# Loading x first, a first block of conditioning on TensorE, 1024-column loads and chunks of 3, 4, 4, 5 in a fused encoder layer

## Chip, core and metric

The kernel runs on one core of one Trainium2 chip. The metric is device microseconds (us) for one execution: the median of several. The engines are TensorE (PE in the profile; PEld is its loading of weights), VectorE (DVE), ScalarE (ACT), GpSimd (POOL) and SyncE (SP), whose queue issues nearly all transfers from HBM. Each engine works through its own queue strictly in order.

## What is computed

One layer on 256 tokens of 2048 channels in float32. The part that matters here is its beginning:

```python
cond = silu(c)                                   # [1, 2048]
mod = cond @ w_mod + b_mod                       # [1, 6*2048]
sh1, sc1, gt1, sh2, sc2, gt2 = split(mod, 6)
u = rms_norm(x, norm1_g) * (1 + sc1) + sh1       # [256, 2048]
aq, ak, av, rq, rf, ri, rg, ga, gr = split_columns(u @ w_in)
ya = diff_attention(aq, ak, av, lam)             # 8 heads
yr = hgrn2(rq, rf, ri, rg, lower_bounds)         # 8 heads, gated recurrence
m = sigmoid(ga) * (ya @ w_att_out) + sigmoid(gr) * (yr @ w_rec_out)
x = x + gt1 * (m @ w_o)
x = x + gt2 * swiglu(rms_norm(x, norm2_g) * (1 + sc2) + sh2)
```

followed by a last RMS norm. `w_mod` has 100 MB, `w_in` 92 MB; all weights together are read once.

## The kernel before

Every product of weights and activations is exact to float32 by splitting both into two parts (`wh`, `wl` and `uH`, `uL`): ScalarE rounds a loaded weight tile to `wh` (line 229), VectorE subtracts to get `wl` (line 231), and TensorE multiplies three times (lines 239 to 241) for each 128 channels ("block"), 512 columns and 128 tokens. With two token tiles a block costs 6 products for 512 columns.

Phase 1 computes seven column groups of `w_in` (`first_cols`: RF, RQ, RI, AQ, AK, AV, RG, each 1024 wide, so 84 products for each of the 16 blocks). A block of `u` needs its scale and shift first, and these need 2048 x 128 values of `w_mod` twice. So phase 1 goes by chunks of blocks (`kchunks`, here 3, 5, 4, 4): while the products of one chunk run, `mod_cols` sums the scales and shifts of the next. It loads rows of `w_mod` (tile `wm`, or `w` for the first chunk), VectorE multiplies them by `cond` and accumulates in `modc` (lines 390 and 394: one instruction for each of 16 row blocks and for scale and shift, 32 in all), TensorE sums `modc` over partitions (`pmc`, line 320, two trace records for each product), VectorE adds the bias (`sh_col`, `sc_col`, lines 403 to 405), and `modulated` makes `u`, `uH` and `uL` (lines 356, 366, 367). How many steps of this go between the products is set by `pace["cond"]`.

`group` does 512 columns at a time in two of the four PSUM banks tagged `acc`; in the first chunk ScalarE copies the banks to `part` (line 434), in later chunks VectorE adds them (line 436). In the last chunk the steps of `hgrn_scores` run beside the products. Phase 2 (the gates, attention, the merge, the SwiGLU) isn't touched.

Before the first chunk the kernel transposes c into `cond`, loads x and normalises it (`norm1`: eight squares on ScalarE, line 328; reciprocal root on VectorE; `xn`, line 343; transposes `pxT`, line 346; copies to `xT`), and loads the small vectors (`rows`, `brows`, lines 142 to 155), which TensorE transposes (`pc`) to give `cols` and `bcols`. The first chunk's loads of `w_mod` stand around the load of x in SP's queue. The tile framework orders the instructions of each engine; buffers rotate: three of `w`, three of `wm`, four each of `wh` and `wl`.

Of the kernel before, what the change touches and what calls it, by code (L numbers as in the profile page):

```python
# [42 lines left out]
XAT, XAT2 = 4, 4  # L43
PACE2, PACE3, PACES, PACE1 = 0.7, 1.6, 2.2, 1.5
kchunks = [(0, 3), (3, 5), (8, 4), (12, 4)]

# column starts of the combined input projection
# [4 lines left out]
def block_kernel(  # L52
# [46 lines left out]
    def make_masks():  # L99
        # mask[L][s, (b, l)] = 1 where key row s lies in the lower half of the 2L-block b  # L100
        for lv in range(7):
            L = 1 << lv
            nb = 64 // L
            m = const.tile([P, 64], F32, name=f"mask{L}")
            nc.gpsimd.memset(m, 1.0)
            mv = m.rearrange("p (b l) -> p b l", l=L)
            nc.gpsimd.affine_select(out=mv, in_=mv, compare_op=ALU.is_ge, fill=0.0,
                                    base=0, pattern=[[-2 * L, nb], [0, L]], channel_multiplier=1)
            nc.gpsimd.affine_select(out=mv, in_=mv, compare_op=ALU.is_ge, fill=0.0,
                                    base=L - 1, pattern=[[2 * L, nb], [0, L]], channel_multiplier=-1)  # L110
            masks[L] = m

# [9 lines left out]
    def quarter(tiles, g):  # L122
        """Columns g*512.. of a row kept in two tiles."""
        return tiles[g // 2][:, (g % 2) * NG:(g % 2 + 1) * NG]
# [37 lines left out]
    def small_params():  # L162
        # lower bound: softmax of the logits over depth, its first cumulative sum
# [12 lines left out]
        # lam on every partition  # L176
# [7 lines left out]
        # lam[:, 0] = lambda, lam[:, 1] = -lambda  # L184
# [4 lines left out]
    def rstd_of(ssq, n, width, name, eps=None):  # L189
        """1 / sqrt(ssq / width + eps), [P, n]: a bit-level first guess and Newton's steps."""  # L190
# [30 lines left out]
    def load_mod(k0, nk, n0, ncol, own):  # L221
        """Rows of w_mod; the first ones go where later the other weights do."""
        return load(w_mod, k0, nk, n0, ncol, wpool.tile([P, nk, ncol], F32, tag="wm", name="wm", bufs=NM) if own else None)

    def split(w, j, n, c0):
        """The parts of w[:, j:j+n, c0:c0+512]."""
# [7 lines left out]
    def products(po, aH, aL, k, wh, wl, kk, first, last, tiles=(0, 1)):  # L234
        """po[t] += a[:, k, t].T @ w[:, kk], in three passes."""
# [19 lines left out]
    def step():  # L255
        """Work beside the products: some of it after every load of weights."""
# [10 lines left out]
    def gemm(ap, kt, n0, aH, aL, k00=0, tail=0):  # L267
        """[256, 512] columns n0.. of a @ w in two banks; the last `tail` channel blocks are done for
        the first 128 tokens before the others."""
# [20 lines left out]
    def halves(tiles):  # L290
        """[P, k, 256] kept in tiles of four k."""
        return lambda k, ts: tiles[k // 4].rearrange("p (k s) -> p k s", s=S)[:, k % 4, ts]

# [1 line left out]
    def mod_rows(name, chunk):  # L295
        """Steps: acc[p, n] = sum over k of cond * w_mod (+ bias on row 0), then its sum over p."""
# [14 lines left out]
    def row_sum(a):  # L311
        """The sums of a's columns, on every partition, in place."""
# [19 lines left out]
    def norm1(xt):  # L332
        s8 = small.tile([P, 2, 4], F32, tag="s8", name="ssq")
        for t in range(2):
            for g in range(4):
                square_sum(s8[:, t, g:g + 1], quarter(xt[t], g))
        s2 = small.tile([P, 2], F32, tag="s2", name="ssq1")
        nc.vector.reduce_sum(out=s2, in_=s8, axis=AX.X)
        rr = rstd_of(s2, 2, D, "n1")
        for g in range(4):  # L340
            for t in range(2):
                xn = tmpt("xn")
                nc.vector.tensor_scalar_mul(out=xn, in0=quarter(xt[t], g), scalar1=rr[:, t:t + 1])
                p = bank("pxT")
                for j in range(4):
                    nc.tensor.transpose(out=p[:, j * P:(j + 1) * P], in_=xn[:, j * P:(j + 1) * P], identity=ident)  # L346
                nc.scalar.copy(out=xT[g].rearrange("p (k s) -> p k s", s=S)[:, :, t * P:(t + 1) * P], in_=p.rearrange("p (k s) -> p k s", s=P))
# [13 lines left out]
    def modulated(src, k, H, L):  # L361
        """H + L = src * sc + sh for the k-th 128 channels."""
# [11 lines left out]
    def mod_cols(k0, nk, chunk, gcol, src, H, L, after=None):  # L374
        """Steps: shift and scale of a norm for channels k0*128.., straight into columns, and then
        the norm's output for these channels."""
        wid = nk * P
        a = [tmp.tile([P, 1024], F32, tag="modc", name=f"modc{ci}", bufs=2) for ci in range(2)]
        own = chunk + k0 > 0
# [19 lines left out]
        for _ in range(GAP if chunk else GAP1):  # L399
            yield  # L400
        ks = slice(k0, k0 + nk)
# [4 lines left out]
        if src is not None:  # L406
            for k in range(k0, k0 + nk):
                modulated(src(k, slice(0, S)), k, H, L)

# [6 lines left out]
    def group(ci, col, g, pieces, last):  # L416
        """Adds the products of pieces (k, nk, parts, column in the parts) to columns col + g*512.."""
        po = [acc_ps.tile([P, NG], F32, tag="acc", name=f"acc{t}") for t in range(2)]
        for i, (k, nk, w, c0) in enumerate(pieces):
            if w is None:  # L420
                w = load(w_in, k, nk, col + g * NG, NG)
            for j in range(0, nk, SK):
                n = min(SK, nk - j)
                wh, wl = split(w, j, n, c0)
                for kk in range(n):
                    products(po, uH, uL, k + j + kk, wh, wl, kk, i == 0 and j + kk == 0,
                             i == len(pieces) - 1 and j + kk == nk - 1)
            step()
        if ci == 0:
            part[col][g] = bigt(f"part{col}").rearrange("p (t n) -> p t n", t=2)  # L430
        for t in range(2):
            d = part[col][g][:, t]
            if ci == 0:
                nc.scalar.copy(out=d, in_=po[t])
            else:
                nc.vector.tensor_add(out=d, in0=po[t], in1=d)
            if last and col == RG:
                nc.scalar.activation(d, d, AF.Sigmoid)

    def mods1(ci):  # L440
        k0, nk = kchunks[ci]
        return mod_cols(k0, nk, 0, g1c, xTv, uH, uL)

    def chunk_cols(ci):
        k0, nk = kchunks[ci]
        full = [(q, 4) for q in range(k0, k0 + nk - nk % 4, 4)]
        rest = nk % 4
        nsteps = 14 * (len(full) + (1 if rest else 0))
        pace["cond"] = 0.0
        if ci + 1 < len(kchunks):  # L450
            cond_side.append(mods1(ci + 1))
            pace["cond"] = AHEAD * 2 * len(mod_loads(kchunks[ci + 1][1])) / nsteps
        last = ci == len(kchunks) - 1
        order = [(col, g) for col in first_cols for g in range(2)]
        if last:
            assert rest in (0, 3)
            order[:4] = [(RF, 0), (RQ, 0), (RF, 1), (RQ, 1)]
        shared = None
        for i, (col, g) in enumerate(order):
            pieces = [(k, n, None, 0) for k, n in full]  # L460
            if rest in (1, 2):
                if g == 0:
                    shared = load(w_in, k0 + nk - rest, rest, col, 1024)
                pieces.insert(len(pieces) if g == 0 else 0, (k0 + nk - rest, rest, shared, g * NG))
            elif rest:
                pieces.append((k0 + nk - rest, rest, None, 0))
            group(ci, col, g, pieces, last)
            if last:
                pace["side"] = PACE1
            if last and (col, g) == (RQ, 0):  # L470
                side.append(hgrn_scores(0))
            if last and (col, g) == (RQ, 1):
# [4 lines left out]
    def transpose4(src):  # L477
        """[128 tok, 4*128] -> a bank [128, 4, 128 tok]."""
# [5 lines left out]
    def split_store(H, L, k0, t, pv, scale=None, bscale=None):  # L484
        """Transposed [128, 4, 128 tok] (in PSUM) times a column -> the parts H, L of k0.."""
# [13 lines left out]
    def normed_heads(po, gate, name, eps=None):  # L499
        """[128 tok, 4 heads, 128] in PSUM -> times rstd per head (and the gate), natural."""  # L500
# [23 lines left out]
    def hgrn_scores(hh):  # L524
        """Four heads. Decays between a query and a key are products of f over the tokens between
        them; a pair is taken at the level L whose 2L-block holds both, in different halves. Within
        L-blocks qa = q times f up to and with the query's token, kb = (1 - f) times f after the
        key's token, T = the product of f over the block."""
# [15 lines left out]
        # the pairs of a token with itself  # L544
# [11 lines left out]
        for lv in range(8):  # L556
# [5 lines left out]
            if L < 128:  # L562
# [5 lines left out]
                # to blocks of twice the length  # L568
# [43 lines left out]
    def attention(hh):  # L612
# [6 lines left out]
        for t in range(2):  # L619
# [3 lines left out]
            for hp in range(2):  # L623
# [16 lines left out]
                # s0 * (p0 / s0 - lam * p1 / s1): the norm of the head takes s0 out again  # L640
# [31 lines left out]
    first = mods1(0)  # L672
    for _ in range(XAT):
        next(first)
    x1 = load_x()
    load_rows()
    for _ in range(XAT2):
        next(first, None)
    norm1(x1)
    for _ in first:  # L680
        pass
    for ci in range(len(kchunks)):
# [202 lines left out]
```

## Time and profile before

| | us |
|---|---|
| median of 3 runs | 1566.48 (1564.33 to 1570.16) |
| profiled execution, span | 1566.1 |
| PE busy in it | 1502.2 (96%) |
| DVE busy | 1105.5 (71%) |
| ACT busy | 729.2 (47%) |

The span is the time from the first to the last instruction of one profiled execution; it is the time of that execution, and lies 0.4 us below the median. Products overlap in the trace (one lasts 390 ns while the next starts earlier), so counts and starts tell more than busy time.

### The profile page before, as it was taken

What the parts mean: (1) busy time and instruction counts of PE and PEld (TensorE: products, weight loads), DVE (VectorE), ACT (ScalarE), POOL (GpSimd) and SP (SyncE); (2) the same over time, 40 slices, a digit from 0 to 9 for tenths busy, and PEclk for the clock granted to TensorE, in tenths of its full rate; (3) what the DMA queues carried; (4) which work ended last, traced back from release to release, by engine and by line L of the source; (5) the groups of instructions that cost most, each with busy time, mean ns of one, the idle gap of its engine ahead of it and who ended that gap; (6) DMA issues with size and microseconds to landing.
All of it is one profiled execution on the core that took longest, in us unless ns stands there. A gap on an engine that the chain in (4) does not pass through costs nothing.

```text
span 1566.1 us, 18325 instructions
## 1 busy us (share of the span) xinstructions
PE 1502.2 (96%) x6931; PEld 1236.2 (79%) x6931; DVE 1105.5 (71%) x1443; ACT 729.2 (47%) x1003; POOL 10.5 (1%) x40
## 2 busy tenths in 40 slices
PE   1989999999999999999989999999999999999997
PEld 1767888888877778788868888788888888888886
DVE  6768889688877688888558877869655444454555
ACT  3554353534466764344345545444333444444443
POOL 1000000000000000000000000000000000000000
PEclk9999999999999999999989999999999999999999
DMA  8888989634664479889648998859655655565652
GB/s 302 284 278 302 311 275 324 206 129 148 232 241 160 135 249 339 312 321 344 206 137 291 334 327 284 315 192 321 205 190 195 194 195 189 190 191 196 207 188 107
DMA packets 175282, 373.67 MB, mean 239 GB/s; under 512 B 8237, under 2 KB 12502, under 8 KB 175194
## 3 DMA queue, kind: packets, MB, share of 16 engines
q1 hardware_dynamic: 174936, 372.42, 69.6%
q8 instruction: 54, 0.88, 0.2%
q14 instruction: 34, 0.28, 0.1%
q10 hardware_dynamic: 258, 0.09, 0.0%
HBM read 370.38 MB, written 2.10 MB: 238 GB/s over the span
## 4 chain that ended last, share of the span: by engine, by line
PE 85%; DVE 6%; DMA 5%; ACT 2%; issue 1%; SPq 0%; ACTq 0%; DVEq 0%
PE acc L239 26%; PE acc L241 26%; PE acc L240 26%; DMA wm<-in_w_mod_dram 3%; PE ptr L481 2%; DVE wl L231 2%; PE pl L566 2%; DVE modc L394 1%; DMA w<-in_w_mod_dram 1%; PE pmc L320 1%; DMA w<-in_w_in_dram 1%; ACT wh L229 1%; DVE gt L305 1%; PE psc L629 0%; PE pxT L346 0%
## 5 line engine op out<-in xcount | busy, mean ns | idle before, releaser
L229 ACT CAST wh<-w 128x1024 fp32r<-128x1024 f32 (+1 forms) x518 | 530.5, 1030 | 693.5 <-PE acc L241 619.0
L231 DVE TENSOR_TENSOR wl<-w,wh 128x1024 fp32r<-128x1024 f32 (+1 forms) x518 | 614.6, 1193 | 327.2 <-ACT wh L229 325.6
L239 PE MATMUL acc<-wh,uH 128*128 128x512 f32 x704 | 278.1, 396 | 6.8 <-ACT wh L229 3.4
L240 PE MATMUL acc<-wl,uH 128*128 128x512 f32 x704 | 277.5, 394 | 2.0 <-DVE wl L231 2.0
L239 PE MATMUL acc<-wh,u2H 128*128 128x512 f32 x704 | 276.2, 392 | 0.8 <-ACT u2H L758 0.8
L241 PE MATMUL acc<-wh,uL 128*128 128x512 f32 x704 | 276.8, 394 | 0.0
L241 PE MATMUL acc<-wh,u2L 128*128 128x512 f32 x704 | 275.6, 391 | 0.0
L240 PE MATMUL acc<-wl,u2H 128*128 128x512 f32 x704 | 274.7, 390 | 0.0
L394 DVE SCALAR_TENSOR_TENSOR modc<-wm,cond,modc 128x512 f32<-128x512 f32 (+2 forms) x180 | 150.4, 857 | 26.4 <-DMA wm<-in_w_mod_dram 25.7
L239 PEld LDWEIGHTS acc<-wh,uH 128*128 128x128 f32 x704 | 133.0, 189 | 35.6 <-ACT wh L229 5.4
L240 PEld LDWEIGHTS acc<-wl,uH 128*128 128x128 f32 x704 | 133.0, 189 | 31.3 <-DVE wl L231 3.1
L241 PEld LDWEIGHTS acc<-wh,uL 128*128 128x128 f32 x704 | 133.1, 189 | 27.9 <-issue 0.6
L239 PEld LDWEIGHTS acc<-wh,u2H 128*128 128x128 f32 x704 | 132.6, 188 | 28.5 <-ACT u2H L758 1.4
L241 PEld LDWEIGHTS acc<-wh,u2L 128*128 128x128 f32 x704 | 132.5, 188 | 27.7 <-DVE u2L L759 0.6
L240 PEld LDWEIGHTS acc<-wl,u2H 128*128 128x128 f32 x704 | 132.6, 188 | 27.5 <-issue 0.2
L240 PE MATMUL acc<-wl,fH 128*128 128x512 f32 x352 | 137.4, 390 | 0.0
L241 PE MATMUL acc<-wh,fL 128*128 128x512 f32 x352 | 137.1, 390 | 0.0
L239 PE MATMUL acc<-wh,fH 128*128 128x512 f32 x352 | 137.0, 389 | 0.0
L305 DVE SCALAR_TENSOR_TENSOR gt<-wm,cond,gt 128x1024 f32<-128x1024 f32 x64 | 81.7, 1277 | 7.6 <-DMA wm<-in_w_mod_dram 7.1
L241 PEld LDWEIGHTS acc<-wh,fL 128*128 128x128 f32 x352 | 66.1, 188 | 13.9 <-issue 0.2
L240 PEld LDWEIGHTS acc<-wl,fH 128*128 128x128 f32 x352 | 66.1, 188 | 13.9 <-issue 0.2
L239 PEld LDWEIGHTS acc<-wh,fH 128*128 128x128 f32 x352 | 66.1, 188 | 13.7
(252 smaller groups left out, 1236.4 us busy)
## 6 DMA issues: line engine op xcount, KB each, us to landing
wm<-in_w_mod_dram SPq DMA_DIRECT2D x160, 512.0 KB, 6.4
w<-in_w_in_dram SPq DMA_DIRECT2D x74, 1024.0 KB, 5.2
w<-in_w_ffn_gate_dram SPq DMA_DIRECT2D x44, 1024.0 KB, 5.2
w<-in_w_ffn_up_dram SPq DMA_DIRECT2D x44, 1024.0 KB, 6.3
w<-in_w_ffn_down_dram SPq DMA_DIRECT2D x44, 1024.0 KB, 5.3
w<-in_w_o_dram SPq DMA_DIRECT2D x16, 1024.0 KB, 6.2
w<-in_w_in_dram SPq DMA_DIRECT2D x14, 768.0 KB, 5.8
wm<-in_w_mod_dram SPq DMA_DIRECT2D x32, 320.0 KB, 4.5
```

Of the source, the lines that this page charges most:

```text
L229: nc.scalar.copy(out=wh, in_=src)
L231: nc.vector.tensor_sub(out=wl, in0=src, in1=wh.bitcast(F32))
L239: mm(po[t], aH(k, ts), h, start=first, stop=False)
L240: mm(po[t], aH(k, ts), lo, start=False, stop=False)
L241: mm(po[t], aL(k, ts), h, start=False, stop=last)
L305: nc.vector.scalar_tensor_tensor(out=a[i], in0=w[:, 0], scalar=cond[:, k:k + 1], in1=a[i], op0=ALU.mult, op1=ALU.add)
L320: mm(p[:, j0 + j:j0 + j + 1], a[:, j * P:(j + 1) * P], ones[:, 0:1], start=True, stop=True)
L394: nc.vector.scalar_tensor_tensor(out=d, in0=w[ci][:, j], scalar=s1, in1=d, op0=ALU.mult, op1=ALU.add)
L481: nc.tensor.transpose(out=p[:, j * P:(j + 1) * P], in_=src[:, j * P:(j + 1) * P], identity=ident)
L566: mm(p[:, (4 * b + j) * 64:(4 * b + j + 1) * 64], kb[:, j, b * P:(b + 1) * P], qb[:, j, b, :, 1, :], start=True, stop=True)
```

## The change

Four things are changed. (1) SP's queue starts with x; the small vectors follow in ScalarE's queue; the squares are shared by ScalarE and VectorE, and the norm is split into `rstd1` and one `norm1` for each 512 columns, with only the first ahead of the rest. (2) The scale and shift of block 0 alone are made by TensorE (`head_loads`, `head_cols`): 2 x 16 products with 128x128 pieces of `w_mod` as weights and a column of `cond` as the moving operand, in place of VectorE's sums. Blocks 1 and 2 go through `mod_cols` as before, with 256 columns at a time in `wm` buffers. (3) `pair` takes the place of `group`: 1024 columns and at most two blocks per load, in all four `acc` banks. (4) Chunks have 3, 4, 4, 5 blocks; the first chunk's products come in pieces of block 0 and blocks 1 to 2.

```diff
-XAT, XAT2 = 4, 4
-kchunks = [(0, 3), (3, 5), (8, 4), (12, 4)]
+kchunks = [(0, 3), (3, 4), (7, 4), (11, 5)]
+HEAD = 1
...
-        own = chunk + k0 > 0
+        own = True
...
+    def head_loads():
+        r = []
+        for ci in (1, 0):
+            w = wpool.tile([P, KT, HEAD * P], F32, tag="w", name="w", bufs=NW)
+            for q in (0, KT // 2):
+                nc.sync.dma_start(out=w[:, q:q + KT // 2], in_=w_mod[q * P:(q + KT // 2) * P, ci * D:ci * D + HEAD * P].rearrange("(k p) n -> p k n", p=P))
+            r.append((ci, w))
+        return r
+    def head_cols(loads):
+        p = bank("pmc")
+        for ci, w in loads:
+            for j in range(HEAD):
+                for q in range(KT):
+                    mm(p[:, ci * HEAD + j:ci * HEAD + j + 1], w[:, q, j * P:(j + 1) * P], cond[:, q:q + 1],
+                       start=q == 0, stop=q == KT - 1)
+        finish_cols(p, 0, HEAD, 0, g1c)
...
+    def pair(ci, col, pieces, last):
+        po = [[acc_ps.tile([P, NG], F32, tag="acc", name=f"acc{t}") for t in range(2)] for g in range(2)]
+        for i, (k, nk) in enumerate(pieces):
+            w = load(w_in, k, nk, col, 1024)
+            for g in range(2):
+                wh, wl = split(w, 0, nk, g * NG)
+                for kk in range(nk):
+                    products(po[g], uH, uL, k + kk, wh, wl, kk, i == 0 and kk == 0, i == len(pieces) - 1 and kk == nk - 1)
+            if k + nk > HEAD:
+                step()
...
-    first = mods1(0)
-    for _ in range(XAT):
-        next(first)
     x1 = load_x()
     load_rows()
-    for _ in range(XAT2):
-        next(first, None)
-    norm1(x1)
-    for _ in first:
+    loads = head_loads()
+    rr = rstd1(x1)
+    norm1(x1, rr, 0)
+    head_cols(loads)
+    for _ in mods1(HEAD, kchunks[0][1] - HEAD):
         pass
+    for g in range(1, 4):
+        norm1(x1, rr, g)
```

ScalarE's queue at the start of the program before (`crow`, `brows`, `rows` are the small vectors; line 131 is the activation that makes `cond`):

```order
L142 DMA brows<-in_b_mod_dram 96x128
L131 ACT_TABLE_LOAD
L131 ACTIVATE cond<-pcond 128x16
L150 DMA rows<-in_norm_g_dram 16x128 x2
L150 DMA rows<-in_lb_logits_dram 16x128
L150 DMA rows<-in_gnorm_g_dram 8x128
L150 DMA rows<-in_subln_g_dram 1x128
```

The same place in the changed kernel:

```order
L142 DMA brows<-in_b_mod_dram 96x128
L328 ACT_TABLE_LOAD
L328 ACTIVATE junk,ssq<-x_114 128x512 x2
L328 ACTIVATE junk,ssq<-x_118 128x512 x2
L131 ACT_TABLE_LOAD
L131 ACTIVATE cond<-pcond 128x16
L150 DMA rows<-in_norm_g_dram 16x128 x2
L150 DMA rows<-in_lb_logits_dram 16x128
L150 DMA rows<-in_gnorm_g_dram 8x128
L150 DMA rows<-in_subln_g_dram 1x128
```

Four squares of x and a second table load have moved ahead of `cond` and of the requests for `rows`.

TensorE's queue at the start, before (`pc` are the transposed small vectors, `pxT` the transposed x, `modc` the sums):

```order
L152 MATMUL pc<-ident,rows 128x57
L153 MATMUL pc<-ident,brows 128x96
L346 MATMUL pxT<-ident,xn 128x128 x32
L320 MATMUL pmc<-ones,modc_114 128x1 x3
L320 MATMUL pmc<-ones,modc_115 128x1 x3
L239 MATMUL acc_304<-wh,uH_104 128x512
```

And in the changed kernel, where line 444 is `head_cols` and 12 products of block 0 (four rows of them shown) follow it:

```order
L152 MATMUL pc<-ident,rows 128x57
L153 MATMUL pc<-ident,brows 128x96
L357 MATMUL pxT<-ident,xn 128x128 x8
L444 MATMUL pmc<-cond,w 128x1 x32
L239 MATMUL acc_348<-wh,uH_104 128x512
L240 MATMUL acc_348<-wl,uH_104 128x512
```

```order
L241 MATMUL acc_351<-wh,uL_108 128x512
L320 MATMUL pmc<-ones,modc_234 128x1 x2
L357 MATMUL pxT<-ident,xn 128x128
L320 MATMUL pmc<-ones,modc_235 128x1 x2
L357 MATMUL pxT<-ident,xn 128x128 x11
L239 MATMUL acc_348<-wh,uH_104 128x512
```

The 32 head products stand between the first transposes and the first products of block 0; the other 24 transposes and the sums of blocks 1 and 2 come after those 12 products.

VectorE's queue in the changed kernel around the end of the head (lines 424 to 426 add the bias for block 0, 405 and 409 are the sums for blocks 1 and 2; before, such sums began as the second instruction of this queue):

```order
L354 TENSOR_SCALAR xn<-x_114,n1y_174 128x512
L171 TENSOR_TENSOR lbz<-lbe 128x8
L424 TENSOR_TENSOR sh_col<-pmc,bcols 128x1
L425 TENSOR_TENSOR sc_col<-pmc,bcols 128x1
L172 RECIPROCAL lbz<-lbz 128x8
L426 SCALAR_TENSOR_TENSOR sc_col<-sc_col,cols 128x1
L173 TENSOR_TENSOR lbc<-lbe,lbz 128x8
L174 TENSOR_SCALAR omlb<-lbc 128x8
L405 TENSOR_SCALAR modc_234<-wm,cond 128x256
L409 SCALAR_TENSOR_TENSOR modc_234<-wm,cond,modc_234 128x256
```

All 32 sums now stand behind line 424, which reads the head's result.

## Rows read from the trace of the kernel before

**Rows 1.** The page's first line.

```profile
span 1566.1 us, 18325 instructions
```

**Rows 2.** By stage: busy PE, PEld, DVE, ACT, POOL; clock, DMA share, GB/s.

```profile
0.00:45.04 45.04, 9.98 (x48) 8.36 (x48) 28.74 (x73) 17.52 (x38) 5.96 (x28) 1.00 0.85 282
45.04:114.41 69.37, 64.15 (x273) 51.38 (x273) 50.05 (x66) 37.03 (x62) 0.00 (x0) 0.95 0.88 303
114.41:213.00 98.59, 97.30 (x432) 79.62 (x433) 82.48 (x117) 43.91 (x58) 0.00 (x0) 1.00 0.82 281
213.00:291.00 78.00, 78.00 (x354) 64.86 (x353) 70.96 (x92) 31.72 (x34) 0.00 (x0) 1.00 0.88 303
```

**Rows 3.** Timeline of the start: start us, us, engine, line, operation, [idle before].

```profile
4.85 0.18 ACT L131 ACTIVATE cond<-pcond 128x16 f32<-128x16 f32 x1 [1.72 <-PE pcond L129]
4.86 0.79 ACTq L150 DMA_DIRECT2D rows<-in_norm_g_dram  x2
...
9.47 0.23 ACTq L150 DMA_DIRECT2D rows<-in_subln_g_dram  x1
...
13.50 0.63 ACT L328 ACTIVATE junk<-x 128x512 f32<-128x512 f32 x1 [8.46 <-DMA x<-in_x_dram]
...
13.94 0.32 PE L152 MATMUL pc<-ident,rows 57*128 57x57 f32 x1 [9.12 <-DMA rows<-in_subln_g_dram]
...
14.25 0.63 ACT L328 ACTIVATE junk<-x 128x512 f32<-128x512 f32 x1
...
17.36 1.28 ACT L169 ACT_TABLE_LOAD   x1
...
32.98 3.80 PE L346 MATMUL pxT<-ident,xn 128*128 128x128 f32 x16 [18.37 <-DVE xn L343]
...
40.95 1.76 PE L320 MATMUL pmc<-ones,modc 128*128 128x1 f32 x12
...
42.75 0.16 DVE L403 TENSOR_TENSOR sh_col<-pmc,bcols 128x3 f32<-128x3 f32 x1 [1.69 <-PE pmc L320]
```

**Rows 4.** Timeline of TensorE at full rate: the first and last of 13 products.

```profile
48.79 0.39 PE L239 MATMUL acc<-wh,uH 128*128 128x512 f32 x1
...
51.55 0.39 PE L239 MATMUL acc<-wh,uH 128*128 128x512 f32 x1
```

**Rows 5.** TensorE's and VectorE's waits, 45.04 to 114.41 us: total, times, longest.

```profile
DVE modc L394 <- DMA wm<-in_w_mod_dram: 11.9, 10, 3.3
...
PE acc L239 <- ACT wh L229: 2.9, 2, 1.5
...
PE acc L240 <- DVE wl L231: 1.3, 1, 1.3
PE acc L239 <- ACT part L434: 1.1, 1, 1.1
```

**Rows 6.** Two short stretches, columns as in rows 2.

```profile
4.00:15.00 11.00, 0.93 (x3) 0.54 (x3) 5.77 (x12) 1.65 (x7) 2.58 (x14) 1.00 1.05 380
...
45.00:49.00 4.00, 3.96 (x10) 3.15 (x11) 3.05 (x6) 1.30 (x3) 0.00 (x0) 0.57 0.95 314
```

**Rows 7.** Instructions on `modc` alone, first chunk: PE's are the sums `pmc`.

```profile
45.04:114.41 69.37, 2.42 (x20) 2.46 (x20) 26.04 (x31) 0.95 0.88 303
```

**Rows 8.** Transfers issued by 60 us: size, us from issue to landing.

```profile
crow<-in_c_dram ACTq DMA_DIRECT2D x1, 8.0 KB, 3.6
rows<-in_lb_logits_dram ACTq DMA_DIRECT2D x1, 8.0 KB, 5.5
```

**Rows 9.** Timeline of VectorE: runs of equal instructions, one behind the other.

```profile
28.36 2.21 DVE L394 SCALAR_TENSOR_TENSOR modc<-w,cond,modc 128x384 f32<-128x384 f32 x4
...
209.78 2.35 DVE L231 TENSOR_TENSOR wl<-w,wh 128x1024 fp32r<-128x1024 f32 x2
...
249.06 2.07 DVE L394 SCALAR_TENSOR_TENSOR modc<-wm,cond,modc 128x512 f32<-128x512 f32 x3
...
252.19 1.28 DVE L436 TENSOR_TENSOR part<-acc,part 128x512 f32<-128x512 f32 x2
```

More of the change, by code (lines that the diff above doesn't have):

```diff
@@ L331, in block_kernel, with rstd1 @@
     xTv = halves(xT)
-    def norm1(xt):
+    def rstd1(xt):
         s8 = small.tile([P, 2, 4], F32, tag="s8", name="ssq")
@@ L335, in norm1 @@
             for g in range(4):
-                square_sum(s8[:, t, g:g + 1], quarter(xt[t], g))
+                if g < 2:
+                    square_sum(s8[:, t, g:g + 1], quarter(xt[t], g))
+                else:
+                    sq = tmpt("sq")
+                    nc.vector.scalar_tensor_tensor(out=sq, in0=quarter(xt[t], g), scalar=1.0, in1=quarter(xt[t], g),
+                                                   op0=ALU.mult, op1=ALU.mult, accum_out=s8[:, t, g:g + 1])
         s2 = small.tile([P, 2], F32, tag="s2", name="ssq1")
         nc.vector.reduce_sum(out=s2, in_=s8, axis=AX.X)
[L339 to L342, printed above, removed]
-                nc.vector.tensor_scalar_mul(out=xn, in0=quarter(xt[t], g), scalar1=rr[:, t:t + 1])
[L344 to L347, printed above, removed]
+        return rstd_of(s2, 2, D, "n1")
+    def norm1(xt, rr, g):
+        for t in range(2):
+            xn = tmpt("xn")
+            if t:
+                nc.scalar.activation(xn, quarter(xt[t], g), AF.Copy, scale=rr[:, t:t + 1])
+            else:
+                nc.vector.tensor_scalar_mul(out=xn, in0=quarter(xt[t], g), scalar1=rr[:, t:t + 1])
+            p = bank("pxT")
+            for j in range(4):
+                nc.tensor.transpose(out=p[:, j * P:(j + 1) * P], in_=xn[:, j * P:(j + 1) * P], identity=ident)
+            d = xT[g].rearrange("p (k s) -> p k s", s=S)[:, :, t * P:(t + 1) * P]
+            if t:
+                nc.scalar.copy(out=d, in_=p.rearrange("p (k s) -> p k s", s=P))
+            else:
+                nc.vector.tensor_copy(out=d, in_=p.rearrange("p (k s) -> p k s", s=P))
     uH_t, uL_t = bigt("uH", F32R, 4), bigt("uL", F32R, 4)
@@ L400, in mod_cols, with finish_cols @@
             yield
+        finish_cols(p, k0, nk, chunk, gcol)
+        if src is not None:
+            for k in range(k0, k0 + nk):
+                modulated(src(k, slice(0, S)), k, H, L)
+    def finish_cols(p, k0, nk, chunk, gcol):
         ks = slice(k0, k0 + nk)
@@ L405, in mod_cols @@
         nc.vector.scalar_tensor_tensor(out=sc_col[:, ks], in0=sc_col[:, ks], scalar=1.0, in1=gcol[:, ks], op0=ALU.add, op1=ALU.mult)
-        if src is not None:
-            for k in range(k0, k0 + nk):
-                modulated(src(k, slice(0, S)), k, H, L)
+    def head_loads():
[14 more added lines that the diff above has]
+        finish_cols(p, 0, HEAD, 0, g1c)
+        for k in range(HEAD):
+            modulated(xTv(k, slice(0, S)), k, uH, uL)
     part = {}
@@ L414, in block_kernel, with mods1 @@
         part[col] = [None, None]
[L416 to L432, printed above, removed]
-            if ci == 0:
[L434 to L441, printed above, removed]
+    def pair(ci, col, pieces, last):
[8 more added lines that the diff above has]
+                step()
+        for g in range(2):
+            if ci == 0:
+                part[col][g] = bigt(f"part{col}").rearrange("p (t n) -> p t n", t=2)
+            for t in range(2):
+                d = part[col][g][:, t]
+                if ci == 0:
+                    nc.scalar.copy(out=d, in_=po[g][t])
+                else:
+                    nc.vector.tensor_add(out=d, in0=po[g][t], in1=d)
+                if last and col == RG:
+                    nc.scalar.activation(d, d, AF.Sigmoid)
+    def mods1(k0, nk):
         return mod_cols(k0, nk, 0, g1c, xTv, uH, uL)
@@ L445, in chunk_cols @@
         k0, nk = kchunks[ci]
-        full = [(q, 4) for q in range(k0, k0 + nk - nk % 4, 4)]
-        rest = nk % 4
-        nsteps = 14 * (len(full) + (1 if rest else 0))
+        pieces = [(k, min(2, k0 + nk - k)) for k in range(k0, k0 + nk, 2)]
+        if ci == 0:
+            pieces = [(0, HEAD)] + [(k, min(2, nk - k)) for k in range(HEAD, nk, 2)]
+        nsteps = len(first_cols) * (len(pieces) - (ci == 0))
         pace["cond"] = 0.0
         if ci + 1 < len(kchunks):
-            cond_side.append(mods1(ci + 1))
+            cond_side.append(mods1(*kchunks[ci + 1]))
             pace["cond"] = AHEAD * 2 * len(mod_loads(kchunks[ci + 1][1])) / nsteps
         last = ci == len(kchunks) - 1
[L454 to L467, printed above, removed]
+        for col in first_cols:
+            pair(ci, col, pieces, last)
             if last:
                 pace["side"] = PACE1
-            if last and (col, g) == (RQ, 0):
+            if last and col == RQ:
                 side.append(hgrn_scores(0))
-            if last and (col, g) == (RQ, 1):
                 side.append(hgrn_scores(1))
```

## The prediction

> **What bounds the kernel now.** I read the page first, then a table by stage, then the timeline of the start, then waits in the first chunk. The profiled execution spans 1566.1 us [rows 1], which is its own time and 0.4 us below the median of 1566.48; the sum below is made against the span. The table by stage [rows 2] shows where TensorE, the bound, is not at work: it is busy for only 9.98 of the first 45.04 us, 64.15 of the next 69.37 (the first chunk), 97.30 of 98.59 in the second chunk and all of 78.00 in the third. So nearly all there is to win lies ahead of 114.4 us: the start, which ends with the first product at 45.04, and the losses of the first chunk.
>
> At full rate products start 0.23 us apart: 12 intervals in 51.55 - 48.79 = 2.76 us [rows 4]. The first chunk has 252 products, 58.0 us. Its 20 records of `pmc` take 2.4 us [rows 7]. TensorE's waits there sum to 2.9 + 1.3 + 1.1 = 5.3 us [rows 5]. The granted clock averages 0.95 over the stage [rows 2], worth 0.05 x 69.4 = 3.5 us; the stretch from 45 to 49 us, right behind the idle start, shows 0.57 [rows 6], nearer the 1.2 GHz level than that of 2.4, and costs 0.43 x 4 = 1.7 us of it. Together 69.2 of 69.37 us: the stage is accounted for.
>
> **The change, part by part.** I follow the changed queues to the time R at which TensorE can start blocks 1 and 2, and from there to the end of the first chunk, which has three blocks before and after, so the two can be compared there.
>
> *x first.* Before, x stood behind three loads of 0.98 MB, and its first square ran at 13.50 us [rows 3]. At 380 GB/s [rows 6] 2.95 MB are 7.8 us, so x now begins at 5.7, and the third of its four loads, two of 0.52 MB later, is there at 8.5. ScalarE's squares start 0.75 us apart (13.50 to 14.25): four are done at 10.0. Then come a table load, 1.28 us, and `cond`, 0.18 us [rows 3]: 11.5 us, where it was made at 4.85 before. That is the price of the new order: the five requests for `rows` follow `cond` in ScalarE's queue. Two take 0.79 us to issue [rows 3], so the last starts about 1.8 us later, at 13.3 (at worst as late as before, 9.47 - 4.85 = 4.6 us after `cond`: 16.1). Before, TensorE had the last of them 4.5 us after its request (13.94 - 9.47); other small transfers took 3.6 to 5.5 [rows 8]. With 4.5, `rows` are there at 17.8.
>
> *The head.* TensorE takes its queue in order: two transposes `pc` (0.7 us by the first's 0.32), eight transposes of x at 3.80 / 16 = 0.24 us [rows 3], then 32 head products. They are of the shape of the `pmc` sums (a full 128x128 float32 weight, one moving column), two records each; 64 records at 2.42 / 20 = 0.121 us [rows 7] are 7.7 us (9.4 at the 1.76 / 12 of the first sums [rows 3]). 17.8 + 0.7 + 1.9 + 7.7 = 28.1 us. Covers: the norm's root on VectorE is ready at about 16 (thirteen tiny operations of some 0.2 us behind squares that end near 13); without that cover the head would wait as long as it is late. The head's 2.1 MB come in pieces of 512 bytes, which no row prices; they follow x, which ends near 8.5 + 1.4 = 9.9, and aren't needed in full until the last quarter of the head begins at 26.2, so only below some 130 GB/s, a third of the row's rate, would they cost anything.
>
> *The sums of blocks 1 and 2* wait in VectorE's queue behind `sh_col` of block 0. Five tiny operations stand there, 0.16 us each [rows 3], so they start at 28.9 although their first weights landed long before; SP's queue, which needs their buffers back, stands still meanwhile. Their width is 256. Four of 384 take 2.21 us and three of 512 take 2.07 [rows 9], 0.55 and 0.69 each, so 0.41 for 256 on the same line (and 0.83 for 640, needed below). 32 are 13.1 us; between them stand one `uL`, also of 256 columns, 0.4, and the splits of the first weights, two of 1024 columns at 2.35 / 2 = 1.18 [rows 9] and two of half that, 3.6 us in all. 46.0 us without a wait. Five of the eight loads can only be asked for once a buffer is released; VectorE's ten waits for such loads in the first chunk cost 11.9 us [rows 5], 1.2 each where they occurred, and the splits cover some: I take 1.0, bounds 0 and 3. 47.0; four records of `pmc` 0.5; then as before 2.3 us from the end of `pmc` (40.95 + 1.76 = 42.71 [rows 3]) to the first product (45.04 [rows 2]); 0.6 for the third set of transposes that now stands ahead of it. R = 50.4. Bounds: 48.5 (small transfers in 3.6, no waits for loads) and 57 (the last request at 16.1 and 5.5 to land, head at 0.147 a record, waits of 3).
>
> *What TensorE has done by R.* The 12 products of block 0 for RF: 12 x 0.23 = 2.8 us, no more, since the next piece in its queue needs blocks 1 and 2. Behind R it owes 240 products, 55.2 us; 16 records of `pmc` for a chunk of four blocks, 1.9; twelve transposes that used to come ahead of the products, 2.9; and one stretch at the low clock, 1.7, since it again sat idle just before. 50.4 + 61.7 = 112.1 us.
>
> *Waits of the first chunk.* The next chunk's conditioning falls from five blocks to four: 8.4 MB in 16 loads in place of 10.5 in 32, so VectorE's loop over three buffers turns half as often, and it does 32 x 0.69 = 22 us of sums where it did 26 [rows 7]. I expect most of the 5.3 us to go: 0.8 left (bounds 0 and 5.3). The chunk ends at 112.9 where it ended at 114.4: 1.5 us won.
>
> *Later chunks.* The second chunk lost 1.3 us before [rows 2]; that goes. The third chunk now prepares five blocks with four blocks of products to cover them. VectorE owes 28 splits at 1.18, 28 additions at 1.28 / 2 = 0.64 [rows 9], 32 sums at 0.83, and some 2 for `uL`: 33.0 + 17.9 + 26.6 + 2 = 79.5 us, against 336 x 0.23 + 2.4 = 79.7 of TensorE. It just fits; before it was 70.96 of 78.00 [rows 2]. I charge 1.2 us for late splits and late emptied banks (bounds 0 and the rival below). Everything behind phase 1 has the same work. Sum: -1.5 - 1.3 + 1.2 = -1.6 us: 1564.5 from the span.
>
> **Rivals.** *Faster, 1557.* If small vectors come at the short end, nothing waits for loads, and the head's records take less than I took, R is near 46; with no waits left in any chunk that is 46 + 61.7 - 114.4 = -6.7, and -1.3: -8.0, 1558; with the loads of 1024 columns smoothing the stages a little further, 1557. For it speaks that transfers do reach 380 GB/s when asked for in time; against it, the fixed order of the queues: `rows`, head, sums follow one another with nothing to overlap. It decides at R = 46.
>
> *Slower, 1577: four banks in one pair.* Before, a group used two of the four `acc` banks, and the other two had a whole group's time to be emptied, 24 products or 5.5 us. Now a pair holds all four, and TensorE wants a bank back 12 products, 2.8 us, after it was filled. VectorE empties two in 1.28 us [rows 9]; with one split (1.18) and one sum (0.69 to 0.83) ahead of them that is 3.2 to 3.3: some 0.5 late, 0.6 with the time until it sees the product's end, in each of 7 pairs of three chunks, 12.6 us: 1577. It decides at 2.8 us between filling and emptying. For it speaks that VectorE was busy at 91% of the third chunk [rows 2]; against it, that its queue puts the additions mostly right behind one split. The Trainium skill says, in Perfetto Trace Analysis, Optimizing Tensor Performance, that independent groups of matmuls should rotate through different PSUM banks so that emptying one overlaps the next group's matmuls; by that rule the old pairing of banks was the better one and this rival would hold. The trace of before can't decide it, since it shows the rotation only, with a total of 1.1 us of waits for an emptied bank in the first chunk [rows 5].
>
> *The change doesn't do what it says.* The early block gives TensorE 2.8 us of work and is otherwise paid for by the sums behind it; at the upper bound R = 56.5 the whole is 1564.5 + 6.6 = 1571, still within 0.5%. This is part of the forecast's own range.
>
> **How the numbers follow.** Within 0.5% (7.8 us, about what a measurement of this kernel can tell from no change) lies the forecast with its range of 1560 to 1572: 0.58. The faster rival with what lies beyond it has 0.20: it needs several bounds at once, but I have worked from queues that I haven't seen running. The slower one has 0.22: the banks at 1577, or R at its upper bound together with the first chunk's waits kept (1571 + 4.5 = 1575.5). The range takes both rivals' nearer ends: 1556 to 1577.
>
> **What would show it.** In the changed profile: `cond` near 11.5 us, the small vectors' transposes near 18, the head's 64 records in 7 to 9 us ending near 28, VectorE's first sum of 256 columns right behind, 12 products of block 0 in the thirties and then an idle TensorE until about 50; the first chunk's end near 112.5. I am wrong if the sums start well before 28 (then the faster rival), if TensorE shows a short wait on the additions to `part` in every pair (the slower one), or if the first chunk still waits for weights.

## The result, and the profile after

The changed kernel takes 1581.56 us (median of 4 runs, 1580.43 to 1582.78), the kernel before 1565.97 beside it: a ratio of 1.0101, with a 95% interval of 1.0083 to 1.0118. It is slower by about 15.6 us, where I forecast 1564.5 and no change to be measured. The profiled execution is the run of 1580.43 us:

```profile
span 1578.5 us, 18439 instructions
```

The start, as a timeline (start, duration, engine, line, operation, count, idle time just before and what ended it); it answers to [rows 3]:

```profile
9.70 0.79 ACTq L150 DMA_DIRECT2D rows<-in_norm_g_dram  x2
...
11.72 0.18 ACT L131 ACTIVATE cond<-pcond 128x16 f32<-128x16 f32 x1
...
13.97 1.61 SPq L218 DMA_DIRECT2D wm<-in_w_mod_dram  x3
...
15.91 0.32 PE L152 MATMUL pc<-ident,rows 57*128 57x57 f32 x1 [11.88 <-DMA rows<-in_lb_logits_dram]
...
18.24 13.65 PE L444 MATMUL pmc<-cond,w 128*128 128x1 f32 x64
...
31.93 0.16 DVE L424 TENSOR_TENSOR sh_col<-pmc,bcols 128x1 f32<-128x1 f32 x1 [13.14 <-PE pmc L444]
...
32.58 0.35 DVE L405 TENSOR_SCALAR modc<-wm,cond 128x256 f32<-128x256 f32 x1
...
35.02 3.51 SPq L218 DMA_DIRECT2D wm<-in_w_mod_dram  x3
...
53.23 1.01 PE L320 MATMUL pmc<-ones,modc 128*128 128x1 f32 x4 [9.37 <-DVE modc L409]
...
58.08 0.78 PE L239 MATMUL acc<-wh,uH 128*128 128x512 f32 x1
```

Read it downwards as one chain. The head's 64 records take 13.65 us, 0.213 us each. VectorE waits 13.14 us for them and only then starts the sums of blocks 1 and 2, whose first weights SP had asked for at 13.97. SP, which needs the buffers back, asks for the next three only from 35.02 on. The sums end at 53.2 and the steady products begin at 58.08: 13 us later than the 45.04 of [rows 2].

The first two rows set a reading of the queues right. The list of ScalarE's queue has the requests for `rows` behind `cond`, and I took them to start after it. They were issued from 9.70 on, and `cond` ran at 11.72: a request did not wait until the activations listed ahead of it were done.

The same by stage, columns as in [rows 2]:

```profile
18.24:25.00 6.76, 6.76 (x34) 6.76 (x33) 0.56 (x3) 1.44 (x4) 0.00 (x0) 1.00 0.58 197
25.00:31.89 6.89, 6.89 (x33) 6.81 (x32) 0.00 (x0) 0.00 (x0) 0.00 (x0) 1.00 0.00 0
...
58.08:117.65 59.57, 59.57 (x270) 49.42 (x268) 46.66 (x61) 37.97 (x55) 0.00 (x0) 1.00 0.89 326
117.65:120.91 3.26, 0.00 (x0) 0.00 (x1) 3.22 (x7) 2.17 (x5) 0.00 (x0) 0.85 0.35 82
120.91:126.66 5.75, 5.22 (x11) 3.63 (x12) 5.15 (x11) 3.14 (x7) 0.00 (x0) 0.50 0.64 248
126.66:213.00 86.34, 86.34 (x390) 71.75 (x389) 76.44 (x103) 36.17 (x40) 0.00 (x0) 1.00 0.82 291
...
213.00:291.00 78.00, 76.79 (x346) 62.69 (x345) 69.36 (x88) 31.81 (x37) 0.00 (x0) 1.00 0.85 299
```

From 25 to 32 us nothing works but TensorE on the head; even the DMA moves 0 GB/s. Then the first chunk runs without any gap to 117.65: the waits of [rows 5] are gone. At its end TensorE stands still for 3.26 us and then works at half clock (0.50) until 126.66. The timeline of that place:

```profile
115.81 1.84 PE L320 MATMUL pmc<-ones,modc 128*128 128x1 f32 x16
...
118.49 0.16 DVE L426 SCALAR_TENSOR_TENSOR sc_col<-sc_col,cols 128x4 f32<-128x4 f32 x1
...
118.68 1.09 ACT L371 ACTIVATE u<-xT,sh_col,sc_col 128x256 f32<-128x256 f32 x2 [1.63 <-DVE sc_col L426]
...
119.68 0.69 ACT L381 CAST uH<-u 128x256 fp32r<-128x256 f32 x2
120.28 0.57 ACT L473 COPY part<-acc 128x512 f32<-128x512 f32 x1
...
120.91 0.79 PE L239 MATMUL acc<-wh,uH 128*128 128x512 f32 x1 [3.26 <-ACT part L473]
...
123.51 0.79 PE L239 MATMUL acc<-wh,uH 128*128 128x512 f32 x1 [0.53 <-ACT part L473]
```

The last pair's four banks were full at 116, but the copies that empty them (line 473) stand in ScalarE's queue behind `u` and `uH` of the next chunk, and `u` waits for `sc_col`, which waits for `pmc`. Two things are late here. The `pmc` of the next chunk run only behind the last product of the first (115.81 to 117.65), so its first `uH`, which takes 0.39 us from 119.68 on, is not there before about 120.1. By this estimate TensorE would have stood still for some 2.4 of the 3.26 us even with all banks empty. The place of the copies behind `u` adds the other 0.8, and the second wait of 0.53.

The twelve product starts from 120.91 to 126.66 take 5.75 us, 0.53 of it the second wait; at full rate they are 2.76 [rows 4].

### The profile page after: what moved, and what is told of

It reads as the page before. It is cut to its first block, busy times and chain, and to the rows that moved or that the text cites. A ratio compares the mean times of both kernels' runs of the same rounds, so it can differ in the third digit from the quotient of the medians.

```text
span 1578.5 us, 18439 instructions
## 1 busy us (share of the span) xinstructions
PE 1519.6 (96%) x6991; PEld 1252.2 (79%) x6991; DVE 1106.2 (70%) x1454; ACT 728.9 (46%) x994; POOL 10.5 (1%) x40
## 4 chain that ended last, share of the span: by engine, by line
PE 82%; DVE 8%; DMA 6%; ACT 2%; issue 2%; SPq 0%; ACTq 0%; DVEq 0%
PE acc L240 25%; PE acc L241 25%; PE acc L239 25%; DMA wm<-in_w_mod_dram 4%; DVE wl L231 3%; PE ptr L507 2%; DVE modc L409 2%; PE pl L592 1%; PE pmc L320 1%; PE pmc L444 1%; DVE gt L305 1%; DMA w<-in_w_in_dram 1%; PE psc L655 1%; ACT wh L229 0%; DMA x<-in_x_dram 0%
## 5 line engine op out<-in xcount | busy, mean ns | idle before, releaser
L409 DVE SCALAR_TENSOR_TENSOR modc<-wm,cond,modc 128x512 f32<-128x512 f32 (+3 forms) x210 | 163.5, 804 | 15.9 <-DMA wm<-in_w_mod_dram 14.7
```

Source lines behind the costliest of these rows:

```text
L409: nc.vector.scalar_tensor_tensor(out=d, in0=w[ci][:, j], scalar=s1, in1=d, op0=ALU.mult, op1=ALU.add)
```

## Experiments

My first theory: the head runs at TensorE's lower clock and everything serial behind it is late (a); the wait at the first chunk's end is the second loss (b). Rivals: summing sixteen products into one column is slow by itself; x first is the cost; pairs and chunks are. All ratios are to runs of the kernel before, on the same chip; the medians of that kernel lie between 1565.97 and 1566.89 us in the four sets of runs, so medians of different rows can be compared within their intervals, some 2 to 4 us to either side.

| run | median us | ratio, 95% interval |
|---|---|---|
| changed kernel | 1581.56 | 1.0101 [1.0083, 1.0118] |
| e1_warm | 1568.50 | 1.0013 [0.9995, 1.0031] |
| e2_own_columns | 1580.98 | one run |
| e3_no_head | 1574.46 | 1.0045 [1.0024, 1.0066] |
| e4_old_start | 1565.87 | 0.9996 [0.9974, 1.0018] |
| e5_warm_sums_behind | 1574.64 | 1.0042 [1.0027, 1.0057] |
| e6_sums_first | 1567.39 | 1.0002 [0.9989, 1.0016] |
| e7_late_step | 1573.84 | 1.0041 [1.0029, 1.0053] |
| e8_sums_first_late_step | 1558.73 | 0.9944 [0.9922, 0.9966] |
| e9_old_start_late_step | 1558.23 | 0.9938 [0.9915, 0.9961] |
| e10_x_first | 1568.69 | 1.0017 [0.9999, 1.0035] |
| e11_e8_warm | 1561.08 | 0.9962 [0.9946, 0.9977] |
| e12_before_3_4_5_4 | 1560.77 | 0.9957 [0.9938, 0.9976] |

**e1_warm.**

```
     x1 = load_x()
+    pwarm = bank("pwarm")
+    for i in range(48):
+        mm(pwarm[:, (i % 4) * P:(i % 4 + 1) * P], ones, ident, start=True, stop=True)
     load_rows()
```

> The changed kernel with 48 products of two constant 128x128 tiles on TensorE, into a spare bank, between the products of the condition (3.8 us) and those of the rows (15.9 us); they change no result. Theory (the head runs at TensorE's 1.2 GHz level because nothing ran before it): its 64 records come 0.12 us apart instead of 0.213, last under 8.5 us instead of 13.65, VectorE's sums start at 26 to 28 us instead of 32.6, the next product after the head block's twelve comes at 51 to 53 us instead of 58.1, and the time is 1574 to 1577 us against 1581.6. Rival (16 products summed into one column of a bank are slow by themselves): 0.21 us apart as before, time within 1.5 us of 1581.6.

It won 13 us, twice what I had expected. Its timeline, and the head's records alone by stretch (TensorE's busy time, VectorE's, clock, DMA):

```profile
4.30 12.41 PE L701 MATMUL pwarm<-ident,ones 128*128 128x128 f32 x96
...
17.85 10.82 PE L444 MATMUL pmc<-cond,w 128*128 128x1 f32 x64
...
42.56 1.01 PE L320 MATMUL pmc<-ones,modc 128*128 128x1 f32 x4 [7.07 <-DVE modc L409]
```

```profile
17.85:20.00 2.15, 2.15 (x20) 2.15 (x21) 0.00 (x0) 1.00 1.08 347
20.00:22.00 2.00, 2.00 (x16) 2.00 (x15) 0.00 (x0) 0.74 0.95 338
...
22.00:28.67 6.67, 6.67 (x32) 6.58 (x31) 0.00 (x0) 0.50 0.83 255
```

The head starts at full clock with 20 records in 2.15 us, 0.11 each; at a clock of 0.50 it has 32 in 6.67 us, 0.21 each, the spacing of the unwarmed head. So the clock sets the spacing, but the head ended only 3.2 us earlier (28.67 for 31.89), while the sums ended 10.7 us earlier (42.56 for 53.23). The rest came from something I hadn't meant to change: the scheduler that orders each engine's queue had moved twelve of VectorE's sums ahead of the head's columns. e5 and e6 take the two apart.

**e2_own_columns.**

```
-                    mm(p[:, ci * HEAD + j:ci * HEAD + j + 1], w[:, q, j * P:(j + 1) * P], cond[:, q:q + 1],
-                       start=q == 0, stop=q == KT - 1)
+                    mm(p[:, ci * KT + q:ci * KT + q + 1], w[:, q, j * P:(j + 1) * P], cond[:, q:q + 1],
+                       start=True, stop=True)
-        finish_cols(p, 0, HEAD, 0, g1c)
+        finish_cols(p[:, ::KT], 0, HEAD, 0, g1c)
```

> The changed kernel with each of the head's 32 products written to a column of its own; the sum over the sixteen pieces is left out, so shift and scale of the first block come from one piece alone. Clock theory: the 64 records stay 0.21 us apart (13.6 us). Rival (summing into one column is what is slow): they come 0.12 to 0.15 us apart (8 to 9.5 us) and the time falls by about 5 us.

This kernel leaves out the sum of the sixteen pieces. The 64 records take 13.65 us again, and the time, of one run, is the same within 1 us: summing into one column is not what is slow. That rival is out.

**e3_no_head.**

```
-    loads = head_loads()
...
-    head_cols(loads)
-    for _ in mods1(HEAD, kchunks[0][1] - HEAD):
+    for _ in mods1(0, kchunks[0][1]):
```

> The changed kernel without the head: VectorE sums the conditioning of all three blocks of the first chunk, in rows 384 wide, as before the change; x first, pairs and the chunks of 3, 4, 4, 5 stay. Theory (the head with what stands behind it is the larger part of the loss, the wait at the first chunk's end the smaller): the last wait before the first chunk's steady products ends at 43 to 47 us instead of 58.1, the wait of 3 us at the chunk's end stays, time 1567 to 1572. Rival 1 (pairs and chunks are the cost): the start gains as much but the time stays over 1575. Rival 2 (x ahead of the weights is the cost): the wait ends after 50 us.

Inconclusive: 7.1 us of the loss went, less than expected. The first product comes at 50.5 us, which is the sign of the second rival (x ahead of the weights is the cost); e10 tries that one by itself. VectorE, no longer held by the head, now waits for weights, 5.6 us in four waits, the longest this one:

```profile
34.99 3.64 DVE L409 SCALAR_TENSOR_TENSOR modc<-wm,cond,modc 128x384 f32<-128x384 f32 x6 [3.25 <-DMA wm<-in_w_mod_dram]
```

In the changed kernel the first chunk's rows of `w_mod` go through the three narrow buffers `wm` (`own = True`), where before they had the wide ones; that this makes the waits is argued, not tried by itself.

**e4_old_start.** Lines 416 to 476 of the kernel before are replaced by `pair` and the new `chunk_cols`, `kchunks` by the new one; the start stays.

> The kernel before with only the loads 1024 columns wide in pairs of groups and the chunks of 3, 4, 4, 5; the old start stays. Theory (two costs): start as before (last wait ends near 45 us), then a wait of 3 to 4 us at the end of the first chunk and a stretch of half clock behind it, 1570 to 1573 us against 1566.0. Rival 1 (all of the loss is in the start): 1565 to 1567. Rival 2 (pairs and chunks are most of it): 1576 or more.

By its time rival 1 held: 1565.87. But the waits are as the theory had them: 3.0 us at the first chunk's end on `part`. Pairs and chunks had therefore won in the first chunk about what they lost at its end; e9 confirms it.

**e5_warm_sums_behind** and **e6_sums_first** separate clock and order. First the diff of e5, which has the 48 products of e1 too and hands the head's last operation on VectorE to the sums, as one that they must follow; then that of e6, where half of the sums are written ahead of the head's columns, and those must follow them.

```
+    pwarm = bank("pwarm")
...
-    head_cols(loads)
-    for _ in mods1(HEAD, kchunks[0][1] - HEAD):
+    fin = head_cols(loads)
+    for _ in mods1(HEAD, kchunks[0][1] - HEAD, fin):
```

> As e1_warm, but VectorE's sums of blocks 1 and 2 are held behind the head's columns, as they stand in the changed kernel; in e1_warm ten or so of them had moved ahead of the head. Theory now (clock and order of VectorE's queue are two costs, and order is the larger): the head takes 10.8 us as in e1_warm, but the last wait before the steady products ends at 53 to 56 us, and the time is 1576 to 1580. Rival (the clock was the cause of all that e1_warm won): that wait ends near 47 us, time 1567 to 1570.

```
+AT = 2
...
+        tc.add_manual_dep(fin.ins, mods["last"].ins.name, NOSYNC, reason="sums first")
...
-    head_cols(loads)
-    for _ in mods1(HEAD, kchunks[0][1] - HEAD):
+    phead = head_products(loads)
+    sums = mods1(HEAD, kchunks[0][1] - HEAD)
+    for _ in range(2 * AT):
+        next(sums)
+    head_cols(phead)
+    for _ in sums:
```

> The changed kernel with 16 of VectorE's 32 sums for blocks 1 and 2 put ahead of the head's columns in its queue; nothing runs on TensorE ahead of the head. Theory (order): the head's records stay 0.21 us apart and end near 32 us, the sums begin before 22 us, SP's next loads of w_mod are asked for near 22 us instead of 35.0, the last wait ends at 46 to 51 us instead of 58.1, time 1569 to 1575. Rival (clock): the wait ends at 55 or later, time over 1578.

e5, timeline:

```profile
18.98 9.73 PE L444 MATMUL pmc<-cond,w 128*128 128x1 f32 x64
...
54.05 0.79 PE L239 MATMUL acc<-wh,uH 128*128 128x512 f32 x1 [0.39 <-ACT uH L381]
```

e6, timeline of three engines:

```profile
18.31 13.65 PE L445 MATMUL pmc<-cond,w 128*128 128x1 f32 x64
...
21.35 4.15 SPq L219 DMA_DIRECT2D wm<-in_w_mod_dram  x3
...
32.00 0.16 DVE L451 TENSOR_TENSOR sh_col<-pmc,bcols 128x1 f32<-128x1 f32 x1 [3.46 <-PE pmc L445]
...
44.73 0.78 PE L240 MATMUL acc<-wh,uH 128*128 128x512 f32 x1
```

With the sums behind the head and a warmer engine the steady products start at 54.05 (4.0 us earlier), and the time is 6.9 us less, a little more than expected. Of the 2.9 us beyond the start, 0.8 are a shorter wait at the chunk's end (2.99 us, once); the rest is within the intervals. With the head as slow as ever and half of the sums ahead of it they start at 44.73 (13.4 earlier), worth 14.2 us, more than expected. VectorE's wait for the head shrinks from 13.14 to 3.46, SP asks for the next weights at 21.35 instead of 35.02. Both costs are real, and order is the larger; e11 asks what the clock still costs once the order is right.

**e7_late_step** and **e8_sums_first_late_step.**

```
-            if k + nk > HEAD:
+            if k + nk > HEAD and i < len(pieces) - 1:
                 step()
...
                 if last and col == RG:
                     nc.scalar.activation(d, d, AF.Sigmoid)
+        step()
...
-            pace["cond"] = AHEAD * 2 * len(mod_loads(kchunks[ci + 1][1])) / nsteps
+            pace["cond"] = (1.4 if ci == 0 else AHEAD) * 2 * len(mod_loads(kchunks[ci + 1][1])) / nsteps
```

This is the diff of e7; e8 has that of e6 as well. It does two things at once: the step of conditioning that followed a pair's last piece now follows the copies of its four banks, and in the first chunk the conditioning goes at a pace of 1.4 in place of `AHEAD`, 1.15.

> The changed kernel with the side step of a pair's last piece behind the emptying of its four banks, and the second chunk's conditioning made one pair earlier. Theory (the four banks stand behind the shift and scale of the next chunk on ScalarE, and the idle time then drops the clock): the waits of 3.26 and 0.53 us at the first chunk's end fall below 1 us in sum, no half clock behind them, the time falls by 4 to 7 us to 1574.5 to 1577.5. Rival (the wait is for the conditioning of the second chunk and only moves): time 1580 or more.

> e6_sums_first and e7_late_step together. Theory: the gains add, 1563 to 1569 us, level with the kernel before (1566) or a little ahead. Rival (something else in pairs and chunks costs 5 us or more): 1572 or more.

e7 gains 7.7 us, a little more than the 4 to 7 expected. The last `pmc` of the second chunk now run ahead of the first chunk's last pair (109.40), where all of them stood behind it (115.81). `u` and `uH` follow the copies of the pair before (109.32) and run beside the last pair's products; the last pair's own copies (116.01, 118.03) still stand behind them, but no longer wait for a late `sc_col`. TensorE's `pmc`, ScalarE, and the table of stages, which shows no idle time and no half clock there:

```profile
109.40 0.95 PE L320 MATMUL pmc<-ones,modc 128*128 128x1 f32 x8
```

```profile
109.32 1.06 ACT L473 COPY part<-acc 128x512 f32<-128x512 f32 x2
110.27 1.06 ACT L229 CAST wh<-w 128x1024 fp32r<-128x1024 f32 x1
111.86 1.09 ACT L371 ACTIVATE u<-xT,sh_col,sc_col 128x256 f32<-128x256 f32 x2 [0.53 <-DVE sc_col L426]
112.86 0.70 ACT L381 CAST uH<-u 128x256 fp32r<-128x256 f32 x2
...
116.01 1.06 ACT L473 COPY part<-acc 128x512 f32<-128x512 f32 x2
...
118.03 1.27 ACT L473 COPY part<-acc 128x512 f32<-128x512 f32 x2
```

```profile
110.00:120.00 10.00, 10.00 (x47) 8.30 (x47) 8.20 (x15) 9.37 (x17) 0.00 (x0) 1.00 0.53 178
120.00:130.00 10.00, 10.00 (x46) 8.23 (x45) 8.06 (x14) 3.40 (x5) 0.00 (x0) 1.00 0.95 354
```

So the loss at the chunk's end is shown, and that the two edits together remove it. Which of them does is not shown, since no run has one alone. Of the rival named ahead of e7 only one half is refuted, that the wait would just move; that the wait is for the second chunk's conditioning holds, by the estimate above, for the larger part of it.

e8 has both: 22.8 us off the changed kernel, the sum of 14.2 and 7.7 within the intervals, and 0.56% faster than the kernel before, beyond the range that I gave.

**e9_old_start_late_step** is e4 with both edits of e7.

> e4_old_start (weights ahead of x, VectorE's sums of all three first blocks, pairs, chunks of 3, 4, 4, 5) with the late step and the earlier conditioning of e7. Theory (the wait at the first chunk's end hid what the wide loads won): 1557 to 1560 us, level with e8_sums_first_late_step, so x first and the head bring nothing even when the order of the sums is right. Rival (the head, rightly ordered, is worth some us): 1563 or more.

1558.23, as the theory has it: with the old start the kernel is as fast as e8. x first and the head bring nothing that can be measured even when rightly ordered; what e8 wins over the kernel before comes from chunks, pairs and the edits of e7. How much of it is the pairs is not shown: e12, with new chunks alone, comes within 2.5 us of e9, and their intervals overlap.

**e10_x_first** sets `XAT, XAT2` from 4, 4 to 0, 8 in the kernel before.

> The kernel before with x, its small vectors and nothing else moved ahead of the conditioning weights; groups, chunks and norm as before. Theory (x first alone costs some 5 us: the sums of VectorE end later and all of the norm waits for it): the first product starts at 48 to 51 us instead of 45.0, time 1569 to 1574. Rival (x first is free, only the head is dear): 45 us, 1565 to 1567.5.

The theory fell. The first product comes at 42.88, ahead of the 45.04 before, and the interval of the time includes 1; 1568.69 lies a little above the rival's range. x first by itself does not delay the start. TensorE's waits in the first chunk are 7.4 us where they were 5.3 [rows 5], so the 2.2 us won at the start are about lost again; the interval leaves room for a loss of up to 0.35%.

```profile
42.88 0.80 PE L239 MATMUL acc<-wh,uH 128*128 128x512 f32 x1 [2.33 <-ACT uH L366]
```

**e11_e8_warm** is e8 with the products of e1.

> e8_sums_first_late_step with the 48 products of e1_warm. Theory (with sums ahead, VectorE's sums end last at the start, not the head): the head ends 3 us earlier, the last wait moves by less than 1.5 us and the time is 1557 to 1560, as e8. Rival (the clock at the start still costs): 1553 to 1556.

No gain: 1561.08, 1 us above the range of the theory and far from the rival's, with an interval that overlaps e8's. The steady products start at 43.28 (44.77 in e8). Once VectorE's sums do not wait for the head, its clock no longer shows in the time.

**e12_before_3_4_5_4** changes one line of the kernel before, `kchunks` to (0, 3), (3, 4), (7, 5), (12, 4).

> The kernel before with chunks of 3, 4, 5, 4 blocks, loads 512 wide as before: only the second chunk's conditioning in the first chunk falls from five blocks to four. Theory (the first chunk's 5.3 us of waits came from the five blocks of conditioning, not from the width of the loads): these waits fall below 1.5 us, the third chunk pays some of it back, time 1560 to 1564. Rival (it is the wide loads): waits of 3 us or more remain, 1565 to 1568.

1560.77, in the range of the theory; the waits fell to 2.0 us, between the two signs (below 1.5, 3 or more). One wait of TensorE is left between 44 and 130 us. ScalarE's rows of the place stand below it:

```profile
PE acc L239 <- ACT part L434: 2.0, 1, 2.0
```

```profile
102.55 0.70 ACT L366 CAST uH<-u 128x256 fp32r<-128x256 f32 x2
...
104.11 1.08 ACT L356 ACTIVATE u<-xT,sh_col,sc_col 128x256 f32<-128x256 f32 x2
105.10 0.69 ACT L366 CAST uH<-u 128x256 fp32r<-128x256 f32 x2
105.70 2.01 ACT L434 COPY part<-acc 128x512 f32<-128x512 f32 x4
```

This wait shows the place of the copies alone: the first `uH` are done at 103.3, and the copies begin at 105.70 behind a second set of `u` and `uH`, with two banks to a group. In e4 and the changed kernel the late `uH` comes on top. TensorE's waits for `wh` and `wl`, 4.2 us in [rows 5], are gone here: the smaller second conditioning ended them, and the wide loads are not needed for it. With one line changed, e12 wins 5.4 us of the 8 that e8 and e9 win.

## Why the prediction was wrong

**Two steps failed.** The first is the term "64 records at 2.42 / 20 = 0.121 us are 7.7 us (9.4 at the 1.76 / 12 of the first sums)". The mechanism was right, the size was not: they took 0.213 each, 13.65 in all. I priced them by rows taken at full clock [rows 7], or nearly so [rows 3], although the same text had [rows 6], a clock of 0.57 behind the idle start. e1 and e2 show that it is the clock and not the form of the sum. The second is the term "0.8 left (bounds 0 and 5.3)" for the waits of the first chunk. It counted waits for weights and put the change to the second chunk at nothing; there the late conditioning, the copies behind it and the half clock after them cost 6.3 us. Without either one of the two the time would have been inside the range: 1574.64 in e5, where the head takes 9.73 us, and 1573.84 in e7.

**R** was 58.08 for 50.4, beyond its upper bound. (That bound was also added up wrong: its four terms give 57.9, not 57, and a later sentence has 56.5.) Of these 7.7 us the head's end is 3.8 (31.89 for 28.1: 5.95 too long, less 1.9 by which `rows` came earlier than forecast, 15.91 for 17.8, since their requests did not wait for `cond`; that was luck), the sums with what stands between them 2.5 (20.65 for 18.1), and the end from the sums to the products 1.5 (4.85 for 3.4, transposes and `pmc` at the lower clock too). That all sums stand behind the head I had read rightly; what I did not work out is what that order costs: e6 shows 13.4 us of R.

**Waits of the first chunk**, 0.8 forecast, bounds 0 and 5.3: right in that the waits for weights went (59.57 of 59.57 us busy), wrong in that new ones of 3.26 and 0.53 us came at the end, with a stretch of half clock behind it (5.75 - 0.53 - 2.76 = 2.5 us). That is 6.3 us seen in the rows; the edits of e7 win 7.7.

**Later chunks.** "That goes" of the second chunk's 1.3 us: right behind the half clock (86.34 of 86.34 busy). The 1.2 us charged to the third chunk: 78.00 - 76.79 = 1.21, a wait of 0.75 us for `wl` at 263.56 and one of 0.46 for an emptied bank at 270.21.

**The slower rival** had a part of the truth: full banks, and the sign. But it put the wait on VectorE, 0.6 us in each of 21 pairs; it was on ScalarE, at the one change of chunks at which ScalarE empties the banks. The rule of the Trainium skill that I set beside it (Perfetto Trace Analysis, Optimizing Tensor Performance: groups rotate through banks, so that emptying overlaps the next group) is met by the order of a queue as much as by the number of banks: e9 fills all four banks in a pair and waits for none at that place, e12 rotates by two and waits 2.0 us.

**The sum.** The profiled span is 14.0 us above the forecast. The first chunk's work ended at 117.65 for 112.9, 4.8 later: 7.7 by R, less the 0.8 of waits that did not come before the end, less 2.1 by which the stretch behind R took 59.57 for 61.7. The chunk's end adds 6.3. The other 3.0 lie in what follows: from 126.66 on, with twelve products of the second chunk done, the program takes 1451.8 us, where the forecast leaves 1564.5 - 112.9 - 2.8 = 1448.8. No row shows where these 3.0 us go; their cause stays open.

## What to carry to other kernels

Price an operation by rows of the same clock: behind an idle start take those of the lower one, and where the text itself has a row of it, ask which terms it reaches. Where one queue serves two consumers, ask what stands behind the instruction that waits: here twelve to sixteen sums put ahead of a waiting operation, or the next chunk's conditioning one pair earlier and behind the copies, were each worth more than what the change was about. And when a small edit moves the time by more than its reason gives, as e1 did, compare the order of the queues before believing the reason.

## What was not expected of the hardware

- TensorE lost its clock while it was busy. In e1 it works without a gap from 4.30 us on, and the granted clock goes from 1.00 to 0.50 within the head, whose products move one column each; their spacing goes from 0.11 to 0.21 us with it. The Trainium skill (TensorE: Matmul & The Clock Gate, What's actually happening) says that the clock follows how busy the engine has been; busy time as the profile counts it did not keep it here.
- The column of the clock shows 1.00 from 18.24 to 31.89 us of the changed kernel, though the records there are 0.213 us apart, as they are at 0.50 in e1. Here the spacing of equal records told the clock, and the column did not.
- The half clock behind a wait of 3.26 us cost 2.5 us more, three quarters of the wait itself.
